# Output projection of a two-layer Conformer/attention trunk: the order of its three passes, and one load of the attention half's weights for two of them

## The chip, the cores and the metric

The kernel runs on one core of a Trainium2 chip. The metric is the device time of one execution in microseconds (us). A core has five engines, each with its own instruction queue that is worked off in order: TensorE (PE, matrix products into the PSUM banks, with its weight loads shown apart as PEld), VectorE (DVE), ScalarE (ACT), GpSimd (POOL) and SyncE (SP, which here only issues DMA transfers). They wait for each other through semaphores.

## The reference

Two layers, 512 tokens, model width 1024. What matters here is the middle of each layer, where the channels of two groups (512 conv channels, 512 attention channels) are joined and projected back to the model width, and the norm and feed-forward block behind it:

```python
for l in range(DEPTH):
    x = x + 0.5 * swiglu(rms_norm(x, ffn1_norm[l]), ...)
    h = rms_norm(x, mix_norm[l])
    a, g, q, k, v = jnp.split(h @ w_in[l], splits, axis=-1)
    conv_out = conv_module(a, g, conv_w[l], conv_b[l], conv_norm[l])
    ...
    diff_out = diff_attention(q, k, v, rel_bias, lam, lam_init, subln_norm[l])
    x = x + jnp.concatenate([conv_out, diff_out], axis=-1) @ w_out[l]
    x = x + 0.5 * swiglu(rms_norm(x, ffn2_norm[l]), ...)
```

`w_out` is 1024 x 1024; its rows 0 to 511 meet the conv channels, rows 512 to 1023 the attention channels. Everything is float32.

## The kernel before

**Layout.** Activations lie transposed: channels on the 128 partitions, tokens along the free dimension. `x` is 8 tiles of 128 channels x 512 tokens, kept on the chip throughout. Attention works through 4 blocks of 128 queries, from block 3 down to block 0 (`steps`, line 932), each block over 4 heads.

**Split products.** Float32 operands are split into a high part of reduced precision (`F32R`) and the remainder, and a product is three matmuls (`mm3`, lines 198 to 204): high x high, high x low, low x high. A raw weight tile of 128 x 512 is loaded into the ring `wraw` (5 entries) by SP, its high part is written by ACT into the ring `whi` and the remainder by DVE or POOL into `wlo` (9 entries each; `parts_of`, lines 99 to 103). `chunk` (line 105) loads and splits two such tiles. In the output projection the remainder is POOL's (the argument `G`, line 1046), and each entry holds the weights of exactly one output tile of 128 channels in one half: the chunk `m // 2`, its entry `m % 2`.

**Order.** The kernel is written against a planner, which follows the written order as a priority, assigns a ring entry or a PSUM bank when an instruction that needs one is placed, and fixes the order of every engine's queue from its own estimate of times. Later work can so be placed ahead of earlier work that isn't ready.

**Around the change.** Attention's last steps (`attend`, line 1008) are, per block: the heads' products with the values (`values`, line 974), squares on ACT (983), a reduction on DVE (985), an addition and a power on POOL (986, 260), scaling on DVE (989), four transposes on PE (1001), and the high and low part of the result into `acth` and `actl` (ACT 1003, DVE 1004). `conv_finish` (line 919) writes the conv channels into tiles 0 to 3 of the same two arrays (POOL 924, ACT 926, DVE 927, ACT 928, DVE 929); attention's four heads are tiles 4 to 7.

The output projection (lines 1042 to 1056) then makes three passes over the eight output tiles `m`: the attention half for tokens 256 to 511 (blocks 2 and 3), the conv half for all tokens, the attention half for tokens 0 to 255 (blocks 0 and 1). Each pass loads and splits its own weights, four chunks, so that those of the attention half are loaded twice. Every output tile of a pass is 4 x 3 matmuls into a bank called `ps_out` (tags `sc` and `po` by turns, two banks each), 256 or 512 columns wide, and an addition on DVE into `x` (line 1051).

`after(m)` prepares tile `m` of `x` for the next norm (`Prep.tile`, line 306: high part on ACT into `acth`, low part on DVE into `actl`, the square on ACT, its sum on DVE). It overwrites tile `m` of `acth` and `actl`, which the projection reads, and so follows the last pass that reads that tile: tiles 0 to 3 are prepared during the third pass, 4 to 7 after it. `first_products` (line 339, called at line 1095) then takes the eight tiles in the order 0 to 7.

Of the kernel before, what the change touches and what calls it, by code (L numbers as in the profile page):

```python
# [20 lines left out]
SEQ = 512  # L21
DM = 1024
KT = DM // P
# [25 lines left out]
    ((10, 18, 15, 19, 16, 20, 17, 21), "last"),  # L49
)  # L50
ORDER = (0, 4, 1, 5, 2, 6, 3, 7)

POOL_TAPS = (TAPS, 0, 0, 10)

# [16 lines left out]
def trunk(ctx: ExitStack, tc: tile.TileContext, xt, par, lamv, relb, onehot,  # L71
          gu1, dn1, wag, wqkv, wout, gu2, dn2, out):
    nc = tc.nc
    V, S, G, T = nc.vector, nc.scalar, nc.gpsimd, nc.tensor
# [14 lines left out]
    def bank(tag, name):  # L89
        return psum.tile([P, 512], F32, tag=tag, name=name, bufs=BANKS[tag])  # L90
# [4 lines left out]
    def ring(tag, n=512):  # L95
        dt = F32R if tag in ("whi", "wlo") else F32
        return wp.tile([P, 512], dt, tag=tag, name=tag, bufs=RING[tag])[:, :n]

    def parts_of(raw, eng=None):
        hi, lo = ring("whi", raw.shape[-1]), ring("wlo", raw.shape[-1])  # L100
        S.activation(hi, raw, AF.Copy)  # L101
        (eng or V).tensor_tensor(out=lo, in0=raw, in1=f32(hi), op=ALU.subtract)  # L102
        return hi, lo

    def chunk(src, eng=None):
        w = []
        for n in range(2):
            raw = ring("wraw")
            nc.sync.dma_start(raw, src[:, n * 512 : (n + 1) * 512])
            w.append(parts_of(raw, eng))  # L110
        return w

    def wpart(w, b, n=P):
        hi, lo = w[b * n // 512]
        c = b * n % 512
        return hi[:, c : c + n], lo[:, c : c + n]
# [31 lines left out]
    class Sums:  # L148

        def __init__(self, load, n=512):  # L150
            self.load, self.n, self.r, self.w = load, n, {}, {}
            for k, first in (("u2u1", "u2"), ("g1u1", "g1")):
                self.r[k] = ring("wsum", n)
                self.get(first, self.r[k], pin=True)
                self.get("u1", self.r[k], add=True)
# [42 lines left out]
    def mm3(ps, w, x, start, stop, pin=False):  # L198
        (wh, wl), (xh, xl) = w, x
        first = T.matmul(ps, wh, xh, start=start, stop=False)  # L200
        if pin:
            tc.keep_in_program_order(first)
        T.matmul(ps, wh, xl, start=False, stop=False)  # L203
        T.matmul(ps, wl, xh, start=False, stop=stop)  # L204
# [58 lines left out]
    def rows_rstd(s, dim, use="", pin=False):  # L263

        ps = bank("y", "ps_rows")
        for j in range(NT):
            mm = T.transpose(ps[:, j * P : (j + 1) * P], s[:, j * P : (j + 1) * P], ident)
            if pin:
                tc.keep_in_program_order(mm)
        v = small.tile([P, NT], F32, tag=f"rowv{use}", name="rowv")  # L270
        V.tensor_reduce(v, ps.rearrange("p (j c) -> p j c", j=NT), axis=AX.X, op=ALU.add)
        V.tensor_scalar(v, v, 1.0 / dim, EPS, op0=ALU.mult, op1=ALU.add)
        return rsqrt(v, NT, use), v
# [24 lines left out]
    class Prep:  # L298


        def __init__(self, l, gain):
            self.l, self.gain = l, gain
            self.hi, self.lo = acth, actl
            self.s = tmp.tile([P, SEQ], F32, tag="ssum", name="ssum", bufs=1)

        def tile(self, k, square=True):
            g = col(self.l, self.gain, k)
            S.activation(self.hi[:, k, :], x[:, k, :], AF.Copy, scale=g)
            V.scalar_tensor_tensor(
                self.lo[:, k, :], x[:, k, :], g, f32(self.hi[:, k, :]), op0=ALU.mult, op1=ALU.subtract  # L310
            )
            if square:
                self.square(k)

        def square(self, k):
            if k == 0:
                S.activation(self.s, x[:, k, :], AF.Square)
            else:
                sq = tmp.tile([P, SEQ], F32, tag="sq", name="sq")
                S.activation(sq, x[:, k, :], AF.Square)  # L320
                V.tensor_tensor(self.s, self.s, sq, op=ALU.add)
# [17 lines left out]
    def first_products(pr, w, ps, early=False, tail=None):  # L339


        if not early:
            rc, v = rows_rstd(pr.s, DM)
            r = spread(rc, "rb", split=True)
        ks = ORDER if tail else range(KT)
        for at, k in enumerate(ks):
            if tail and at == TAIL_AT:
                tail()
            if early and not tail and at == STATS_AT:
                rc, v = rows_rstd(pr.s, DM, pin=True)  # L350
            for i in range(2):
                mm3(ps[0][i], wpart(w[0][i], k), pr[k], at == 0, at == KT - 1,
                    pin=early and (at in (0, STATS_AT) or tail))
        for i in range(2):
            for at, k in enumerate(ks):
                if tail and at == i == 0:
                    rc, v = rows_rstd(pr.s, DM, pin=True)
                if early and i == 0 and at == STATS_AT + (2 if tail else 0):
                    r = spread(rc, "rb", pin=True)
                mm3(ps[1][i], wpart(w[1][i], k), pr[k], at == 0, at == KT - 1,  # L360
                    pin=early and at in (0, STATS_AT, STATS_AT + 2))
        return rc, v, r
# [221 lines left out]
    def begin(pr, loads, tail=None):  # L584
        ws = [[chunk(src) for src in pair] for pair in loads]
        ps = [pair_banks() for _ in loads]
        return [*zip(ws, ps)], first_products(pr, ws, ps, early=tail is not None, tail=tail)
# [184 lines left out]
    def mixer(l, pr, after, begun):  # L772
        with tc.tile_pool(name="mix", bufs=1) as mp, tc.tile_pool(name="mt", bufs=2) as mt:
# [101 lines left out]
            ch, cl = acth, actl  # L875
# [163 lines left out]

            for half, t in ((1, slice(SEQ // 2, SEQ)), (0, slice(0, SEQ)), (1, slice(0, SEQ // 2))):
                w = [None] * 4
                for m in range(KT):
                    if w[m // 2] is None:
                        w[m // 2] = chunk(wout[l, half, m // 2], G)
                    ps = bank(("sc", "po")[m % 2], "ps_out")[:, : t.stop - t.start]
                    for kk in range(4):
                        k = half * 4 + kk
                        mm3(ps, wpart(w[m // 2], (m % 2) * 4 + kk), (ch[:, k, t], cl[:, k, t]), kk == 0, kk == 3)  # L1050
                    V.tensor_tensor(x[:, m, t], ps, x[:, m, t], op=ALU.add)

                    if half == 1 and t.start == 0 and m < KT // 2:
                        after(m)
            for m in range(KT // 2, KT):
                after(m)


    pr = Prep(0, "ffn1_norm")
    for k in range(KT):  # L1060
# [12 lines left out]
    for l in range(DEPTH):  # L1073
        nxt = {}

        def preparing(gain, l2=l):
            def after(m):
                if m == 0:
                    nxt["p"] = Prep(l2, gain)
                nxt["p"].tile(m)  # L1080
            return after

        def store(m):
            nc.sync.dma_start(out[m], x[:, m, :])

        def store_half(n, half, queue):
            queue.dma_start(out[KT - 1][:, n * HS : (n + 1) * HS], half)

        with tc.tile_pool(name="ffn", bufs=1) as fp:
            begun = ffn(fp, pr, gu1[l], dn1[l], preparing("mix_norm"), begun,  # L1090
                        lambda tail: begin(nxt["p"], [[wag[l, c, i] for i in range(2)] for c in range(2)], tail),
                        (l == 0, 1), aside if l == 0 else None)
        mixer(l, nxt["p"], preparing("ffn2_norm"), begun)
        with tc.tile_pool(name="ffn", bufs=1) as fp:
            begun = begin(nxt["p"], [[gu2[l, m, i] for i in range(2)] for m in range(2)])
            if l + 1 < DEPTH:
                begun = ffn(fp, nxt["p"], gu2[l], dn2[l], preparing("ffn1_norm", l + 1), begun,
                            lambda tail: begin(nxt["p"], [[gu1[l + 1, m, i] for i in range(2)] for m in range(2)], tail), (0, 1))
            else:
                ffn(fp, nxt["p"], gu2[l], dn2[l], store, begun, lambda tail: tail(store_half), (0, 0), end=True)  # L1100
        pr = nxt["p"]
# [74 lines left out]
```

## Time and profile before

| | |
|---|---|
| time, median of 3 runs | 1770.37 us (1769.22 to 1770.41) |
| the profiled execution's own time | 1772.28 us |
| its span, first to last instruction | 1770.5 us |
| output projection of layer 0 in it | about 495 to 544 us from the span's start |
| output projection of layer 1 in it | about 1374 to 1423 us |
| DVE, ACT and POOL busy | 83%, 59% and 29% of the span |
| moved by DMA | 257.79 MB, 146 GB/s on average |

A row of the profile that begins with a line number is a group of instructions of that line of the kernel: engine, operation, tile written <- tiles read, count. The views quoted below are: busy time by window (a stretch in us from the span's start, its length, then for each engine its busy time and the instructions in it, the granted clock of PE as a share, the DMA engines' busy share and GB/s), one tile's instructions (count, least/median/most duration in ns, first and last start in us, shapes), and the timeline (start in us, duration in us). Matmuls overlap in PE's pipeline: a matmul's duration is longer than the pace at which they follow each other. A few matmul records are missing in a trace.

### The profile page before, as it was taken

The page shows a single profiled execution, that of the slowest core. Times are in us where ns is not written, and L with a number is a line of the kernel's source. Part 1 is how long each engine was busy: PE and PEld are TensorE (multiplying, and loading weights), DVE is VectorE, ACT ScalarE, POOL GpSimd, SP SyncE. Part 2 cuts the span into 40 slices and gives each one's busy share as a digit, 9 for nine tenths or more (in the row PEclk, how much of TensorE's full clock was granted, in tenths as well). Part 3 has the DMA queues.
Part 4 walks back from the last instruction along what each step waited for, and adds up shares of the span by engine and source line. Part 5 has one row for each costly group of instructions (what it writes and reads, how often), then busy time and mean ns, then how long its engine had stood idle before and what let it go on. Part 6 is the DMA issues. An engine that isn't in the chain of part 4 may idle for free.

```text
span 1770.5 us, 33000 instructions
## 1 busy us (share of the span) xinstructions
PE 1758.8 (99%) x11852; PEld 1620.9 (92%) x11852; DVE 1470.9 (83%) x2646; ACT 1037.4 (59%) x1955; POOL 516.1 (29%) x497
## 2 busy tenths in 40 slices
PE   9999999999999999999999999999999999999998
PEld 7799999988788899999988999999887888999998
DVE  7969888969877869899977798899698678698887
ACT  6546565755855446566644565666559554465664
POOL 1111112169970011112200121121798600111122
PEclk9999999999999999999999999999999999999999
DMA  7457777533223447677543576776231234576774
GB/s 230 128 140 188 172 194 177 145 112 102 66 84 108 134 123 186 162 202 179 145 142 103 152 182 172 192 162 177 81 113 49 100 105 135 132 184 171 193 179 126
DMA packets 166614, 257.79 MB, mean 146 GB/s; under 512 B 19271, under 2 KB 63318, under 8 KB 166448
## 3 DMA queue, kind: packets, MB, share of 16 engines
q1 hardware_dynamic: 129600, 201.25, 35.3%
q0 software_dynamic: 36416, 54.12, 18.6%
q8 instruction: 93, 1.52, 0.3%
q14 instruction: 73, 0.60, 0.1%
q10 hardware_dynamic: 432, 0.29, 0.1%
HBM read 253.48 MB, written 3.42 MB: 145 GB/s over the span
## 4 chain that ended last, share of the span: by engine, by line
PE 94%; DVE 2%; DMA 1%; POOL 1%; ACT 1%; issue 1%; DVEq 0%; ACTq 0%; SPq 0%; POOLq 0%
PE ps_pair L434 36%; PE ps_pair L523 16%; PE ps_pair L200 9%; PE ps_pair L203 9%; PE ps_pair L204 9%; PE ps_out L200 2%; PE ps_out L203 2%; PE ps_out L204 2%; PE ps_pair L829 2%; PE ps_pair L828 2%; PE ps_pair L827 2%; PE ps_sc L944 1%; PE ps_v L858 1%; PE ps_v L859 1%; PE ps_v L857 1%
## 5 line engine op out<-in xcount | busy, mean ns | idle before, releaser
L101 ACT ACTIVATE whi<-wraw 128x512 fp32r<-128x512 f32 x744 | 452.5, 627 | 409.1 <-PE ps_pair L203 170.0
L102 DVE TENSOR_TENSOR wlo<-wraw,whi 128x512 fp32r<-128x512 f32 x640 | 426.3, 685 | 110.1 <-ACT whi L101 97.5
L160 POOL DMA_DIRECT2D wsum<-in_gu x128 | 112.0, 914 | 701.1 <-DMA wsum<-in_gu 279.2
L434 PE MATMUL ps_pair<-acth,wlo 128*128 128x256 f32 x1024 | 289.8, 283 | 0.0
L434 PE MATMUL ps_pair<-actl,whi 128*128 128x256 f32 x1024 | 289.8, 283 | 0.0
L434 PE MATMUL ps_pair<-acth,whi 128*128 128x256 f32 x1024 | 289.8, 283 | 0.0
L434 PE MATMUL ps_pair<-th,whi 128*128 128x256 f32 x768 | 217.3, 283 | 0.0
L434 PE MATMUL ps_pair<-tl,whi 128*128 128x256 f32 x768 | 217.3, 283 | 0.0
L434 PE MATMUL ps_pair<-th,wlo 128*128 128x256 f32 x768 | 217.3, 283 | 0.0
L200 PE MATMUL ps_pair<-acth,whi 128*128 128x512 f32 x512 | 200.0, 393 | 0.3 <-DVE gs L642 0.3
L203 PE MATMUL ps_pair<-actl,whi 128*128 128x512 f32 x512 | 199.5, 390 | 0.0
L204 PE MATMUL ps_pair<-acth,wlo 128*128 128x512 f32 x512 | 199.3, 390 | 0.0
L434 PEld LDWEIGHTS ps_pair<-actl,whi 128*128 128x128 f32 x1024 | 196.6, 192 | 0.2
L434 PEld LDWEIGHTS ps_pair<-acth,whi 128*128 128x128 f32 x1024 | 196.6, 192 | 0.2
L434 PEld LDWEIGHTS ps_pair<-acth,wlo 128*128 128x128 f32 x1024 | 196.6, 192 | 0.0
L160 POOL DMA_DIRECT2D wsum<-in_dn x112 | 98.8, 1120 | 271.4 <-DMA wsum<-in_dn 46.3
L102 DVE TENSOR_TENSOR wlo<-wsum,whi 128x512 fp32r<-128x512 f32 x192 | 130.0, 683 | 23.7 <-ACT whi L101 23.4
L434 PEld LDWEIGHTS ps_pair<-th,whi 128*128 128x128 f32 x768 | 147.5, 192 | 0.0
L434 PEld LDWEIGHTS ps_pair<-tl,whi 128*128 128x128 f32 x768 | 147.5, 192 | 0.0
L434 PEld LDWEIGHTS ps_pair<-th,wlo 128*128 128x128 f32 x768 | 147.5, 192 | 0.0
L523 PE MATMUL ps_pair<-hh,whi 128*128 128x256 f32 x512 | 145.0, 283 | 1.6 <-ACT keep L530 1.6
L102 POOL TENSOR_TENSOR wlo<-wraw,whi 128x512 fp32r<-128x512 f32 x104 | 137.0, 1339 | 31.2 <-ACT whi L101 19.0
(209 smaller groups left out, 4460.8 us busy)
## 6 DMA issues: line engine op xcount, KB each, us to landing
wraw<-in_gu SPq DMA_DIRECT2D x280, 256.0 KB, 3.4
wsum<-in_gu SPq DMA_DIRECT2D x128, 256.0 KB, 3.8
wsum<-in_gu POOLq DMA_DIRECT2D x128, 256.0 KB, 4.6
wraw<-in_dn SPq DMA_DIRECT2D x68, 256.0 KB, 3.4
wraw<-in_wqkv SPq DMA_DIRECT2D x48, 256.0 KB, 2.6
wraw<-in_wout SPq DMA_DIRECT2D x48, 256.0 KB, 2.7
wraw<-in_dn SPq DMA_DIRECT2D x64, 128.0 KB, 3.7
wraw<-in_wag SPq DMA_DIRECT2D x32, 256.0 KB, 2.9
```

Source lines behind the costliest of these rows:

```text
L101: S.activation(hi, raw, AF.Copy)
L102: (eng or V).tensor_tensor(out=lo, in0=raw, in1=f32(hi), op=ALU.subtract)
L160: nc.gpsimd.dma_start(dst[:, to], src, accum_op=ALU.add)
L200: first = T.matmul(ps, wh, xh, start=start, stop=False)
L203: T.matmul(ps, wh, xl, start=False, stop=False)
L204: T.matmul(ps, wl, xh, start=False, stop=stop)
L434: mm = T.matmul(ps, l, r, start=first and i == j == 0, stop=False, skip_group_check=True)
L523: mm = T.matmul(ps, s[:, f], r, start=side not in self.begun, stop=False, skip_group_check=True)
L827: T.matmul(ps[n], xh[:, t], wh, start=k == 0, stop=False)
L828: T.matmul(ps[n], xh[:, t], wl, start=False, stop=False)
L829: T.matmul(ps[n], xl[:, t], wh, start=False, stop=k == KT - 1)
L857: T.matmul(ps, xh[:, t], wh, start=k == 0, stop=False)
```

## The change

The passes become: the attention half for tokens 256 to 511, the attention half for tokens 0 to 255, the conv half. The dictionary of weights now spans all passes, so the second pass uses the tiles of the first. The conv half takes output tiles 4 to 7 first, then 0 to 3 (`LATER`), and so does `first_products` where it has no `tail`. Tiles 4 to 7 are prepared for the next norm during the conv half, tiles 0 to 3 behind it. Since tile 0 is no longer the first to be prepared, the norm's sum is begun by whichever square comes first, and `preparing` makes its `Prep` at the first call.

```diff
+LATER = (4, 5, 6, 7, 0, 1, 2, 3)
...
             self.s = tmp.tile([P, SEQ], F32, tag="ssum", name="ssum", bufs=1)
+            self.squares = 0
...
         def square(self, k):
-            if k == 0:
+            self.squares += 1
+            if self.squares == 1:
                 S.activation(self.s, x[:, k, :], AF.Square)
...
-        ks = ORDER if tail else range(KT)
+        ks = ORDER if tail else LATER
...
-            for half, t in ((1, slice(SEQ // 2, SEQ)), (0, slice(0, SEQ)), (1, slice(0, SEQ // 2))):
-                w = [None] * 4
-                for m in range(KT):
-                    if w[m // 2] is None:
-                        w[m // 2] = chunk(wout[l, half, m // 2], G)
+            w = {}
+            for half, t in ((1, slice(SEQ // 2, SEQ)), (1, slice(0, SEQ // 2)), (0, slice(0, SEQ))):
+                for m in range(KT) if half else LATER:
+                    if (half, m // 2) not in w:
+                        w[half, m // 2] = chunk(wout[l, half, m // 2], G)
                     ps = bank(("sc", "po")[m % 2], "ps_out")[:, : t.stop - t.start]
                     for kk in range(4):
                         k = half * 4 + kk
-                        mm3(ps, wpart(w[m // 2], (m % 2) * 4 + kk), (ch[:, k, t], cl[:, k, t]), kk == 0, kk == 3)
+                        mm3(ps, wpart(w[half, m // 2], (m % 2) * 4 + kk), (ch[:, k, t], cl[:, k, t]), kk == 0, kk == 3)
                     V.tensor_tensor(x[:, m, t], ps, x[:, m, t], op=ALU.add)
-
-                    if half == 1 and t.start == 0 and m < KT // 2:
+                    if half == 0 and m >= KT // 2:
                         after(m)
-            for m in range(KT // 2, KT):
+            for m in range(KT // 2):
                 after(m)
...
         def preparing(gain, l2=l):
+            made = []
+
             def after(m):
-                if m == 0:
-                    nxt["p"] = Prep(l2, gain)
-                nxt["p"].tile(m)
+                if not made:
+                    made.append(Prep(l2, gain))
+                    nxt["p"] = made[0]
+                made[0].tile(m)
             return after
```

## The prediction

> **What bounds the kernel now.** I read the page's span and busy shares first.
>
> ```profile
> span 1770.5 us, 33000 instructions
> ## 1 busy us (share of the span) xinstructions
> PE 1758.8 (99%) x11852; PEld 1620.9 (92%) x11852; DVE 1470.9 (83%) x2646; ACT 1037.4 (59%) x1955; POOL 516.1 (29%) x497
> ```
>
> TensorE (PE) lacks 11.7 us of being busy for the whole span. Time can be won only by closing one of its gaps, and it is lost at once when a new gap opens. So I went to the stretch that the change touches and asked for the busy time by window. The rows are, for layer 0: the end of attention, the output projection, the opening of the second feed-forward block; and the output projection of layer 1.
>
> ```profile
> core 0: us, PE busy (x) PEld busy (x) DVE busy (x) ACT busy (x) POOL busy (x), PEclk, DMA share, GB/s
> 485.00:495.10 10.10, 9.07 (x65) 7.75 (x65) 9.81 (x41) 8.53 (x30) 5.19 (x6) 1.00 0.01 2
> 495.10:544.05 48.95, 48.90 (x318) 44.49 (x319) 34.48 (x69) 29.90 (x61) 29.53 (x23) 1.00 0.33 108
> 544.07:585.00 40.93, 40.93 (x184) 33.81 (x183) 30.94 (x55) 17.33 (x28) 1.92 (x2) 1.00 0.35 114
> 1374.30:1423.20 48.90, 48.87 (x318) 44.45 (x319) 34.40 (x69) 29.84 (x61) 28.98 (x23) 1.00 0.32 109
> ```
>
> Three things are to be seen. The projection already keeps PE busy for 48.90 of 48.95 us, at full clock. What follows it has no gap at all. And the two layers' projections repeat each other within 0.05 us, with as many instructions on each engine, so one layer's sum may be doubled.
>
> **What the change moves.** The three passes of the projection lie thus in the trace (busy time of the instructions on the tile ps_out alone):
>
> ```profile
> 495.10:511.86 16.76, 15.17 (x103) 1.00 0.14 47
> 511.86:532.55 20.69, 20.50 (x91) 1.00 0.43 140
> 532.55:544.07 11.52, 11.52 (x97) 1.00 0.42 138
> ```
>
> The first is the attention half for tokens 256 to 511, mixed with the last heads of attention; the second is the conv half; the third the attention half for tokens 0 to 255. The change swaps the second and the third. All 288 matmuls stay with their widths: 96 in the third pass, 11.52/96 = 0.12 us each; in the conv half, 20.69 us less 0.35 for four transposes, over 89 = 0.23 us each. **Matmul work: 0.**
>
> **What it removes.** The weights of the attention half are no longer loaded twice: per layer 8 loads of 256 KB, 8 ScalarE splits, 8 GpSimd subtractions.
>
> ```profile
> L101 ACT ACTIVATE whi<-wraw x15: 615/627/632, 498.7 to 529.9; 128x512 fp32r<-128x512 f32 x15
> L102 POOL TENSOR_TENSOR wlo<-wraw,whi x15: 1286/1299/1751, 505.1 to 530.6; 128x512 fp32r<-128x512 f32 x15
> L109 SPq DMA_DIRECT2D wraw<-in_wout x10: 327/328/328, 506.5 to 521.2; - x10
> ```
>
> (From the view of the raw weight tiles between 495 and 532 us; durations are least, median, most in ns.) That is 8 x 0.63 = 5.0 us of ACT, 8 x 1.30 = 10.4 us of POOL and 8 issues of 0.33 us on SP's queue per layer, all inside the windows above in which PE doesn't wait. **On the path: 0.** The cover is PE's own 48.9 us; without it a split would be owed to whoever waited for it, up to 0.63 + 1.30 us, but the rows show nobody.
>
> **What it adds: a wait for the last attention block.** Queries are worked off from block 3 down to block 0, and tokens 0 to 255 need blocks 1 and 0. In the kernel before, the conv half stands between. Block 0's way to its output appears in the view of the tile ps_o (PE's last values product is L974; of L1003 and L1004 the last start counts) and in that of the tile so:
>
> ```profile
> L1001 PE MATMUL ps_o<-ident,ov x4: 270/272/272, 521.2 to 521.5; 128*128 128x128 f32 x4
> L974 PE MATMUL ps_o<-vv,at x2: 270/272/273, 510.2 to 510.3; 128*128 128x128 f32 x2
> L1003 ACT ACTIVATE acth<-ps_o,gsub x2: 669/679/689, 510.5 to 521.8; 128x512 fp32r<-128x512 f32 x2
> L1004 DVE SCALAR_TENSOR_TENSOR actl<-ps_o,gsub,acth x2: 736/744/751, 512.3 to 522.5; 128x512 fp32r<-128x512 f32 x2
> L974 PEld LDWEIGHTS ps_o<-vv,at x1: 187/187/187, 510.2 to 510.2; 128*128 128x128 f32 x1
> L983 ACT ACTIVATE sq<-ps_o x1: 579/579/579, 512.7 to 512.7; 128x512 f32<-128x512 f32 x1
> L989 DVE TENSOR_TENSOR ov<-ps_o,rs_y x1: 692/692/692, 518.7 to 518.7; 128x512 f32<-128x512 f32 x1
> ```
>
> ```profile
> L985 DVE TENSOR_REDUCE so<-sq x1: 671/671/671, 513.7 to 513.7; 128x4 f32<-128x512 f32 x1
> L986 POOL TENSOR_TENSOR so<-so,se x1: 198/198/198, 517.4 to 517.4; 128x4 f32<-128x4 f32 x1
> L260 POOL TENSOR_TENSOR rs_y<-so,mhalf x1: 1006/1006/1006, 517.7 to 517.7; 128x4 f32<-128x4 f32 x1
> ```
>
> Block 0 is ready at 522.5 + 0.75 = 523.3 us, 11.4 us after the conv half began and 9.2 us before its consumer starts: hidden now. But much of that way is queueing which the change takes away. POOL was at this, by its timeline,
>
> ```profile
> 505.13 12.31 POOL L102 TENSOR_TENSOR wlo<-wraw,whi 128x512 fp32r<-128x512 f32 x8
> ```
>
> when the reduction ended at 513.7 + 0.7 = 514.4, and L986 stood 3.0 us behind it. Those eight weights are split later in the new order, since the ring of nine split weight tiles keeps eight for their second use until pass two runs. L983 began 2.1 us after L974's end (510.6), L1001 1.8 us after L989's (519.4). The durations from L983 to L1003 alone add to 0.58 + 0.67 + 0.20 + 1.01 + 0.69 + 0.6 + 0.69 = 4.4 us. With ordinary hand-overs the way can be read off block 2, before POOL's run (L983's first start, L1004's last):
>
> ```profile
> L1004 DVE SCALAR_TENSOR_TENSOR actl<-ps_o,gsub,acth x2: 748/748/749, 488.3 to 496.0; 128x512 fp32r<-128x512 f32 x2
> L983 ACT ACTIVATE sq<-ps_o x2: 586/586/587, 488.8 to 496.5; 128x512 f32<-128x512 f32 x2
> L989 DVE TENSOR_TENSOR ov<-ps_o,rs_y x1: 681/681/681, 492.5 to 492.5; 128x512 f32<-128x512 f32 x1
> L1003 ACT ACTIVATE acth<-ps_o,gsub x1: 687/687/687, 494.4 to 494.4; 128x512 fp32r<-128x512 f32 x1
> ```
>
> From 488.8 to 495.1 are 6.3 us to the high part, to 496.7 are 7.9 us to the low one. Put behind L974's end at 510.6: ready at 516.9 and 518.5 as the late end. The early end is the bare 4.4 us, with the last head as much earlier as the conv matmuls that PE ran before it took (next paragraph, 1.6 us): 510.6 - 1.6 + 4.4 = 513.4.
>
> **What PE has to do meanwhile.** The view of ps_out for the first-pass window holds
>
> ```profile
> L200 PE MATMUL ps_out<-acth,whi x35: 278/283/682, 495.2 to 511.5; 128*128 128x256 f32 x32, 128*128 128x512 f32 x3
> L203 PEld LDWEIGHTS ps_out<-actl,whi x34: 188/192/192, 497.2 to 511.5; 128*128 128x128 f32 x34
> L203 PE MATMUL ps_out<-actl,whi x34: 280/283/401, 497.3 to 511.6; 128*128 128x256 f32 x32, 128*128 128x512 f32 x2
> L204 PEld LDWEIGHTS ps_out<-acth,wlo x34: 187/191/192, 497.4 to 511.6; 128*128 128x128 f32 x34
> L204 PE MATMUL ps_out<-acth,wlo x34: 279/283/396, 497.5 to 511.7; 128*128 128x256 f32 x32, 128*128 128x512 f32 x2
> ```
>
> Seven conv matmuls, the 512-wide ones (7 x 0.23 = 1.6 us), are in it: the planner already takes ready conv work ahead of unfinished attention work, and gives it an output bank. It can do so afterwards too, but only for one output tile of twelve matmuls: each output tile uses one ring entry, and eight of nine are held. So PE has 511.86 + 5 x 0.23 = 513.0, and with L1001's transposes (0.35 of pace) 513.35 us. A second conv tile comes after a split of 0.63 + 1.30 us in the freed entry, from about 514.9 on, if the planner puts it there.
>
> **The gap.** PE is free at 513.35; the high part is ready between 513.4 and 516.9: 0 to 3.6 us. The low part follows 1.6 us later by block 2's rows; the first matmul of each of four open output tiles (0.12 us each) covers 0.5 us, so up to 1.1 us more. Per layer 0 to 4.7 us. I take 2.4: nearer the middle, because the hand-overs of block 2 apply, while the freed ACT and POOL let the last head finish earlier. What is queued behind the wait are pass two, the rest of the conv splits (their entries come free tile by tile), and everything after; nothing of it is shortened later, so PE's gap goes to the end. DVE's evictions and the norms have slack.
>
> **What is late or early next.** In the second pass, conv weights are split as entries free, every 1.44 us, against POOL's 1.30: seven by its end, and PE then takes one per 2.7 us. **0.** At the end, the conv half's output tiles leave every 2.7 us instead of 1.44, so DVE's work for the next norm (add, two preparations, one weight split, about 0.7 us each, 2.8 together) spreads wider. Tiles 0 to 3 must wait for the last conv matmul, as tiles 4 to 7 now wait for the last attention matmul; the products take them in the order 4 to 7, 0 to 3, four tiles (5.4 us) later. There was no gap (40.93 of 40.93 us), so **0** either way. The counters in the norm code change which square is written first, not how many.
>
> [...] The longest idle time of PE in this trace is in these windows,
>
> ```profile
> 1751.30:1753.40 2.10, 0.03 (x1) 0.00 (x0) 2.04 (x4) 2.07 (x5) 0.00 (x0) 1.00 0.05 10
> 1753.40:1760.00 6.60, 6.58 (x55) 6.58 (x55) 6.42 (x13) 2.32 (x5) 0.00 (x0) 1.00 0.20 79
> ```
>
> and the clock granted after it is 1.00. [...]
>
> **The sum.** 0 + 0 + 2 x 2.4 = +4.8 us: profiled execution 1772.28 (span 1770.5 and 1.8 around it) becomes 1777.1. That execution stands 1.9 us above the median of the runs shown, 1770.37, so the forecast is 1770.4 + 4.8 = 1775.2 us; with the ends, 1770.4 to 1779.8.
>
> **Rivals.** *Hidden after all: not slower.* The last head's values product is planned earlier, since ACT's splits between 498 and 514 are gone, or the second conv tile fills the gap. Mechanism: block 0 is ready by 513.9, a gap of 0.5 us or less, 2 x 0.5 = +1.0: 1771.4. It decides from 0.2% (3.5 us, about what a measurement of this kernel tells from no change), that is a gap under 1.75 us per layer. For it: the queueing counted above. Against: 6.3 us in the only undisturbed block.
>
> *No filler: much slower.* Pass two's four output tiles hold all four banks while they wait, or no conv weights are split in time. PE then stops at 511.86 - 1.6 + 0.35 = 510.6, block 0 comes at 516.9 - 1.6 = 515.3, low part 1.1 beyond the cover: 5.8 us per layer, +11.6: 1782.0. [...] Against it: the seven early conv matmuls.
>
> *Faster.* It could come only from gaps in these windows: 10.10 - 9.07 and 48.95 - 48.90 are 1.08 us per layer, 2.2 in all, so 1768.2 at best; the ones before 495.1 lie ahead of anything that changes. Over 0.2% would need gaps elsewhere, such as the 2.1 us above, to close by a different plan.
>
> **How the numbers follow.** Forecast (gap of 1.75 to 4.7 us) 0.50; hidden or equal 0.31; no filler 0.12; faster by over 0.2% 0.07. Slower by over 0.2% is 0.50 + 0.12 = 0.62, within 0.31, faster 0.07. The likeliest case's own range is 1773.9 to 1779.8. The range for 8 in 10 leaves the faster case and the upper part of the no-filler case out, half in ten each: 1769.0 to 1783.0.
>
> **What would show it.** Right: in both layers a PE gap before the first 256-wide matmul of the second pass, ended by ACT's L1003 (high part) or DVE's L1004; some twelve 512-wide matmuls ahead of it; POOL idle before L986; 32 loads of in_wout in all; no gap after the pass order's end. Wrong on filler: no 512-wide ps_out matmul before the gap. Wrong altogether: PE busy through the second pass's start, or a gap at the conv half or at the next block's first products, which I price at nothing.

## The result, and the profile after

| | before | after |
|---|---|---|
| median of 5 runs each, taken together | 1769.22 us (1768.66 to 1770.41) | 1782.06 us (1781.27 to 1783.26) |
| ratio after to before, 95% interval | | 1.0071 [1.0059, 1.0082] |
| profiled execution | 1772.28 us | 1781.82 us |

The change costs 12.8 us. The busy shares of the changed kernel:

```profile
span 1780.0 us, 32900 instructions
## 1 busy us (share of the span) xinstructions
PE 1763.6 (99%) x11852; PEld 1625.2 (91%) x11852; DVE 1469.8 (83%) x2646; ACT 1034.1 (58%) x1939; POOL 492.6 (28%) x481
```

ACT and POOL have 16 instructions fewer each (the splits of both layers), PE as many as before. PE's busy time is nevertheless 4.8 us longer: some matmuls took longer than they did before. It isn't one execution's accident: the mean granted clock of the changed kernel is 0.996 or 0.997 in each of its five runs, and 0.999 or 1.000 in every later run of the kernel before.

Busy time by window, in the columns shown in the prediction: for each layer the projection, then the opening of the next feed-forward block.

```profile
495.60:550.60 55.00, 50.76 (x318) 46.15 (x319) 36.68 (x75) 28.92 (x57) 17.36 (x15) 0.97 0.21 68
550.60:591.50 40.90, 40.90 (x183) 33.80 (x182) 31.13 (x55) 17.56 (x29) 2.84 (x3) 1.00 0.38 115
1379.05:1434.90 55.85, 51.62 (x320) 46.77 (x321) 37.02 (x76) 29.25 (x57) 17.36 (x15) 0.94 0.21 69
1434.90:1475.90 41.00, 41.00 (x184) 33.91 (x183) 31.20 (x55) 17.33 (x28) 2.84 (x3) 1.00 0.39 113
```

All of the loss is in the projection. From its first matmul to the first one of the next block it now takes 54.96 us in layer 0 (495.67 to 550.63) and 55.48 us in layer 1, where it took 48.91 us in both. That is 6.05 + 6.57 = 12.6 of the 12.8 us. The feed-forward block opens without a gap, as before. Two things are new in the projection's rows: 4.2 us in which PE isn't busy, and a granted clock of 0.97 and 0.94.

PE's timeline of layer 0, from the end of the first pass to the first matmuls of the second (start, duration, and in brackets the idle time before and what ended it):

```profile
510.64 0.28 PE L205 MATMUL ps_out<-acth,wlo 128*128 128x256 f32 x1
514.31 0.63 PE L1004 MATMUL ps_o<-ident,ov 128*128 128x128 f32 x4 [3.39 <-DVE ov L992]
515.72 1.22 PE L201 MATMUL ps_out<-acth,whi 128*128 128x256 f32 x4 [0.78 <-ACT acth L1006]
516.74 0.41 PE L204 MATMUL ps_out<-actl,whi 128*128 128x256 f32 x1
```

PE runs dry at 510.92 and waits twice: 3.39 us for block 0's scaled values (its lines are three higher now: 989 is 992, 1001 is 1004, 1003 is 1006), then, behind the four transposes, 0.78 us for the high part. No 512-wide matmul stands before or between. A matmul lasts 0.28 us where the next would have followed after 0.12, so each gap costs some 0.16 us more than its idle time: 3.55 + 0.94 = 4.5 us. Layer 1 has the same two gaps, 3.39 and 0.78 us.

The other part of the loss is the clock. These rows are cut where the granted clock changes, and at the same spacing before:

```profile
508.91:512.33 3.42, 2.01 (x18) 1.81 (x16) 3.05 (x7) 1.90 (x3) 0.59 (x2) 1.00 0.00 0
512.33:515.74 3.41, 0.65 (x5) 0.44 (x5) 0.98 (x3) 0.69 (x1) 1.11 (x1) 1.00 0.02 5
515.74:519.15 3.41, 3.41 (x16) 3.41 (x17) 0.71 (x1) 0.04 (x1) 0.00 (x0) 0.50 0.00 0
519.15:522.57 3.42, 3.42 (x30) 3.42 (x30) 1.27 (x3) 1.86 (x3) 2.61 (x3) 1.00 0.09 32
...
1392.96:1396.38 3.42, 1.40 (x12) 1.20 (x11) 3.06 (x6) 1.45 (x3) 1.20 (x2) 1.00 0.00 0
1396.38:1399.79 3.41, 1.26 (x5) 0.89 (x6) 0.88 (x2) 0.69 (x1) 0.50 (x1) 0.50 0.00 0
1399.79:1403.21 3.42, 3.42 (x17) 3.42 (x18) 0.56 (x1) 0.20 (x1) 0.00 (x0) 0.50 0.00 0
```

Just when block 0 has come, the clock is halved for 3.41 us: 16 matmuls go through where the next window takes 30. In layer 1 it is halved for two such windows, in the first of which PE was mostly idle anyway. The projection's extra time less the gaps puts the half clock at 6.05 - 4.5 = 1.6 us in layer 0 and 6.57 - 4.5 = 2.1 us in layer 1, a short wait for the low part among it. So the sum of the loss is 2 x 4.5 us for the gaps and 3.6 us for the clock; the run "Warm through the gap" below gives some 0.6 of the 3.6 us back to the waits.

Why did nothing fill the gap? The order in which PE executed the projection's matmuls tells it, read from the timelines of layer 0 (width, count and pass; attention's own matmuls are left out). A view names the operands, not the number of an output tile.

```
before                                  after
(pass one goes on)                      (pass one goes on)
512 x1   conv half, at 504.95           256 x12  pass one, at 509.25
256 x12  pass one                       (idle 3.39, block 0's transposes, idle 0.78)
512 x1   conv half, at 506.62           256 x4   pass two, at 515.72, the first
256 x12  pass one, at 507.11                     matmuls of four output tiles
512 x5   conv half                      256 x92  pass two
256 x12  pass one, at 510.35            512 x96  conv half, at 528.84
512 x89  conv half, at 511.86
256 x96  third pass, at 532.55
```

What follows is read off the kernels, and the next two runs test it. Banks of one tag are handed out in the written order. In the kernel before, the conv half was the written next user of `sc`, so its first tile got a bank while 36 matmuls of pass one, three output tiles' worth, were still to come. In the changed kernel the written next users of all four banks are tiles 0 to 3 of pass two. They take them and wait for block 0, and the conv half stands behind them, its first tile too, which the next run shows to be ready.

### The profile page after: what moved, and what is told of

Its sections match the earlier page's. It is cut to its first block, busy times and chain, and to the rows that moved or that the text cites. A ratio compares the mean times of both kernels' runs of the same rounds, so it can differ in the third digit from the quotient of the medians.

```text
span 1780.0 us, 32900 instructions
## 1 busy us (share of the span) xinstructions
PE 1763.6 (99%) x11852; PEld 1625.2 (91%) x11852; DVE 1469.8 (83%) x2646; ACT 1034.1 (58%) x1939; POOL 492.6 (28%) x481
## 5 line engine op out<-in xcount | busy, mean ns | idle before, releaser
L102 ACT ACTIVATE whi<-wraw 128x512 fp32r<-128x512 f32 x728 | 444.1, 628 | 410.8 <-PE ps_pair L204 172.6
L526 PE MATMUL ps_pair<-hl,whi 128*128 128x256 f32 x512 | 144.9, 283 | 0.0
L526 PE MATMUL ps_pair<-hh,wlo 128*128 128x256 f32 x512 | 144.9, 283 | 0.0
```

The costliest lines, as they stand in the source:

```text
L526: mm = T.matmul(ps, s[:, f], r, start=side not in self.begun, stop=False, skip_group_check=True)
```

## The experiments

In the expectations, A is the theory held at that time, and the other letters are its rivals, with the numbers that each would give. The kernel before was run again with each of the three groups: 1769.97 us (18 runs; bank, written, warm and reload), 1769.74 us (17 runs; two tiles, shared only and the kernel before) and 1769.61 us (21 runs; the last two).

**One conv tile with a bank of another tag.** The changed kernel, but the conv half's first tile takes the idle bank `y` instead of its turn for `sc`.

```diff
-                    ps = bank(("sc", "po")[m % 2], "ps_out")[:, : t.stop - t.start]
+                    tag = "y" if half == 0 and m == KT // 2 else ("sc", "po")[m % 2]
+                    ps = bank(tag, "ps_out")[:, : t.stop - t.start]
```

> The changed kernel with one edit: the conv half's first output tile (m = 4) takes the bank y instead of sc. Theory A (banks handed out in written order keep conv work out of the gap): PE works off 12 conv matmuls of 0.227 us, 2.7 us, before block 0 is ready; the 3.39 us gap shrinks to about 0.7 us with the 0.78 us behind it, the granted clock stays 1.00, the loss per layer is 1.5 us: about 1772 us. Rival B (the planner keeps written order, or the conv half isn't ready): order and time unchanged, 1782 us.

Measured: 1773.98 us, ratio 1.002 [1.0011, 1.0029]: 8.1 us are won back by a name of a bank. Its PE timeline at the same place:

```profile
513.09 0.39 PE L205 MATMUL ps_out<-acth,wlo 128*128 128x512 f32 x1
514.09 0.66 PE L1004 MATMUL ps_o<-ident,ov 128*128 128x128 f32 x4 [0.61 <-DVE ov L992]
515.52 0.74 PE L201 MATMUL ps_out<-acth,whi 128*128 128x256 f32 x4 [0.78 <-ACT acth L1006]
```

The filler that the prediction had counted on, twelve 512-wide matmuls, now stands ahead of the transposes. PE runs on to 513.48, where the prediction had 513.0. Gaps of 0.61 and 0.78 us are left, the clock stays full (behind the gaps of layer 0 a 256-wide matmul lasts 0.28 us, where the changed kernel had 0.41), and the projection takes 51.08 us in both layers. The time is 2 us above the expectation; the two gaps, 0.61 + 0.78 + 2 x 0.16 = 1.7, are most of the 2.2 us per layer that remain.

**One conv tile written ahead of pass two.** The same filler by the other way: its bank stays `sc`, but its turn comes earlier.

```diff
-            for half, t in ((1, slice(SEQ // 2, SEQ)), (1, slice(0, SEQ // 2)), (0, slice(0, SEQ))):
-                for m in range(KT) if half else LATER:
+            for half, t, ms in ((1, slice(SEQ // 2, SEQ), range(KT)), (0, slice(0, SEQ), LATER[:1]),
+                                (1, slice(0, SEQ // 2), range(KT)), (0, slice(0, SEQ), LATER[1:])):
...
+                for m in ms:
...
```

The lines left out keep the preparation of that tile for the next norm behind pass two.

> The changed kernel with conv output tile m = 4 written ahead of the second pass, in its usual bank. Theory A: its turn for a bank of sc comes before the second pass's, so it fills the gap as in the run with bank y: about 1772 us. Rival B (conv not ready in time, its inputs or weights late): PE waits for conv first, 1780 us or more.

Measured: 1774.28 us, ratio 1.0025 [1.0015, 1.0035], with the same 51.08 us in both layers. In the first run the written order stayed and a bank was free; in this one the banks stayed and the turn came earlier. Either is enough, so what the conv tile lacked was a bank at its turn, and neither its inputs nor its weights.

**Warm through the gap.** The changed kernel, with twelve matmuls of a constant into another bank behind the first pass; nothing reads their result. They do no work of the projection, but keep PE busy.

```diff
+                if t.start:
+                    idle = bank("tp", "ps_idle")
+                    with behind(mm):
+                        for _ in range(12):
+                            T.matmul(idle, ones_r, ones_r.unsqueeze(1).broadcast_to([P, NT, P]), start=True, stop=True)
```

Here `mm` is the last matmul of the first pass.

> The changed kernel with 12 matmuls on constants (512 wide, 0.227 us each, 2.7 us, their result unused) behind the first pass. They do no work of the kernel, so the wait for block 0 stays. Theory A (the gap of 3.39 us is paid once, and half clock for 3.4 us in layer 0 and 6.8 us in layer 1 is paid on top): granted clock 1.00 throughout, 1.7 + 3.4 = 5.1 us less: 1777 us. Rival C (the half clock falls on time that PE would have waited anyway): 1782 us.

Measured: 1780.03 us (1778.94 to 1782.14), ratio 1.0057 [1.0045, 1.007], between the two expectations. The profiled execution is the slowest of the five. In it layer 0 kept its clock and took 53.91 us instead of 54.96; layer 1 lost it for one window and took 55.40 instead of 55.48. The windows of layer 1:

```profile
1396.75:1400.17 3.42, 1.84 (x11) 1.23 (x11) 1.44 (x2) 0.69 (x1) 0.08 (x1) 1.00 0.00 0
1400.17:1403.59 3.42, 3.42 (x18) 3.42 (x18) 0.42 (x1) 0.63 (x1) 0.66 (x1) 0.50 0.00 0
```

Block 0 comes no sooner here: its transposes start 514.94 - 496.14 = 18.80 us after the projection's first matmul in layer 0, against 514.31 - 495.67 = 18.64 us in the changed kernel. The half clock is thus a cost of its own. The other four runs bear it out: their mean granted clock is 1.000, where a single window at half clock (half of 3.41 us, of some 1780) would leave 0.999, and they took 1778.94 to 1780.85 us, by their median 2.3 us less than the changed kernel. The expectation had set the cost too high, and had taken for granted that the clock would be kept in both layers of every run.

The size comes out below 3.6 us, too. Layer 0, at full clock, still takes 53.91 - 48.91 = 5.0 us more than before, 0.16 of them by the later transposes. So the waits alone cost some 4.8 us per layer instead of 4.5. The 0.3 between is mostly PE's wait for the low part:

```profile
516.34 0.74 PE L201 MATMUL ps_out<-acth,whi 128*128 128x256 f32 x4 [0.78 <-ACT acth L1006]
517.13 0.39 PE L204 MATMUL ps_out<-actl,whi 128*128 128x256 f32 x1
```

The first matmul with the low part starts 0.79 us after the first with the high part, and the four of the high part fill only 4 x 0.12 = 0.48 of it. In the changed kernel it starts 1.02 us after (516.74 less 515.72), of which the four fill 0.85 at half clock: the slower pace hides a part of that wait. By this estimate, from one layer of one execution, the half clock costs 6.05 - 4.8 = 1.2 and 6.57 - 4.8 = 1.8 us, 3.0 in all.

**The new order with the weights loaded anew.** The changed kernel, but each pass loads and splits its own weights, as before.

```diff
             for half, t in ((1, slice(SEQ // 2, SEQ)), (1, slice(0, SEQ // 2)), (0, slice(0, SEQ))):
+                w = {}
```

> The changed kernel, but each pass loads and splits its own weights again (24 loads per layer, no tile held for two passes). Theory A (the order of the passes is the cause, the shared load no part of it): the gap stays, and POOL's splits for the second pass again stand before block 0's small operations, up to 5 us later per layer: 1782 to 1795 us. Rival D (keeping eight of nine ring entries is what stops the conv half from filling in): 1769 to 1773 us.

Measured: 1793.97 us, ratio 1.0136 [1.0121, 1.0152]: the loss is the order's, and sharing the weights takes half of it away. PE's and POOL's timelines:

```profile
519.31 1.09 PE L1004 MATMUL ps_o<-ident,ov 128*128 128x128 f32 x4 [8.52 <-DVE ov L992]
521.17 1.22 PE L201 MATMUL ps_out<-acth,whi 128*128 128x256 f32 x4 [0.78 <-ACT acth L1006]
```

```profile
505.15 10.95 POOL L103 TENSOR_TENSOR wlo<-wraw,whi 128x512 fp32r<-128x512 f32 x7
516.06 0.20 POOL L989 TENSOR_TENSOR so<-so,se 128x4 f32<-128x4 f32 x1
```

The gap is 8.52 us, because block 0's small addition on POOL stands behind seven splits. This is the queueing that the prediction saw before the change (L986, 3.0 us behind such a run) and expected to go; it goes only with the second load.

**Two conv tiles as filler.** The changed kernel with tiles 4 and 5 in banks `y` and `tp`, and three ring entries of their own for the conv half's weights (the third argument of `chunk`, handed on to `parts_of`).

```diff
...
-                        w[half, m // 2] = chunk(wout[l, half, m // 2], G)
-                    ps = bank(("sc", "po")[m % 2], "ps_out")[:, : t.stop - t.start]
+                        w[half, m // 2] = chunk(wout[l, half, m // 2], G, None if half else mp)
+                    tag = {4: "y", 5: "tp"}.get(m) if half == 0 else None
+                    ps = bank(tag or ("sc", "po")[m % 2], "ps_out")[:, : t.stop - t.start]
```

> The changed kernel with two conv output tiles free to fill the wait: tile 4 takes bank y, tile 5 bank tp, and the conv half's split weights have three ring entries of their own. Theory A (all of the change's loss is PE's missing work while block 0 is unfinished): 24 conv matmuls, 5.4 us, cover the 3.4 + 0.8 us, no gap over 0.8 us in the projection, clock 1.00: 1769.5 to 1771 us, the time before. Rival B (something else of the change costs time too, at its end or through the wider output tiles): as with one tile, 1773 us or more.

Measured: 1775.05 us, ratio 1.003 [1.0019, 1.004]. A miss: with twice the filler no better than with one tile.

```profile
517.99 0.60 PE L1007 MATMUL ps_o<-ident,ov 128*128 128x128 f32 x4
519.37 0.74 PE L204 MATMUL ps_out<-acth,whi 128*128 128x256 f32 x4 [0.78 <-ACT acth L1009]
```

The planner put all 24 conv matmuls ahead of block 0's transposes, so the 3.39 us are closed, but nothing is left for the 0.78 us behind them. By the medians 1775.05 - 1769.74 = 5.3 us are lost: 2 x (0.78 + 0.16) = 1.9 in this gap, and 3.0 that the next run loses, too.

**Shared weights alone.** The order of before, but the attention half's weights loaded once, and the conv half's in three entries of their own (in the passes' loop `w = {}` once, the key `(half, m // 2)`, and the third argument of `chunk` as above).

> The kernel before, its order of passes unchanged, with the weights of the attention half loaded once for both of its passes and three ring entries of their own for the conv half. It does what the change removes, without what it adds. Theory A (the 16 loads, 16 ACT splits and 16 POOL subtractions lie under busy PE): 1769 to 1771 us, no difference. Rival E (they cost time on the path, about 0.3 us per split weight tile where PE waits): 1765 us or less.

Measured: 1772.77 us, ratio 1.0016 [1.0007, 1.0025], 3.0 us more than the kernel before. A miss by 2 us. POOL's timeline around block 2:

```profile
480.14 2.53 POOL L105 TENSOR_TENSOR wlo<-wraw,whi 128x512 fp32r<-128x512 f32 x2
482.61 2.65 POOL L902 TENSOR_TENSOR yp<-yp,prod 128x512 f32<-128x512 f32 x2
...
493.33 0.21 POOL L989 TENSOR_TENSOR so<-so,se 128x4 f32<-128x4 f32 x1
```

With free entries, two more splits are placed in the midst of attention, where DVE, ACT and POOL have work that PE waits for. That this is the cause wasn't shown by this run. The theory after it: the entries cost something only where their splits are made early.

**The kernel before once more.** One more execution, because the first profile has gaps of 1.58 us near 1099 and 2.09 us near 1751, the second of them quoted in the prediction.

> The kernel before once more, unchanged. Theory A (the two gaps of 2.09 us and 1.58 us in its first profile belong to that execution, not to the plan): they are gone or elsewhere and the time is near 1770 us. Rival F (they are planned waits that the change removed): both are there again and the time is near 1772 us.

Measured: 1768.83 us. Its windows at both places, and those of the first profile:

```profile
1095.00:1103.00 8.00, 8.00 (x69) 8.00 (x68) 7.31 (x14) 4.51 (x10) 1.76 (x2) 1.00 0.82 209
1740.00:1757.00 17.00, 16.65 (x139) 16.45 (x138) 13.18 (x24) 7.22 (x15) 3.31 (x4) 1.00 0.56 131
```

```profile
1095.00:1103.00 8.00, 6.42 (x54) 6.22 (x53) 5.00 (x10) 3.80 (x8) 1.97 (x3) 1.00 0.80 179
1740.00:1757.00 17.00, 14.91 (x125) 14.71 (x123) 11.58 (x20) 5.86 (x13) 3.57 (x4) 1.00 0.56 134
```

Both gaps belong to that one execution, not to the kernel; what made them wasn't followed up. Together, 3.67 us, they are about what the first profile took more than this one (1772.28 less 1768.83 is 3.45). Held against this execution, the changed kernel's profiled one takes 1781.82 - 1768.83 = 13.0 us more, as the medians say; against the first it is only 9.5.

**Two tiles, with their work held back.** The changed kernel with tiles 4 and 5 in `y` and `tp` and one entry for tile 5's weights; its split is held behind `conv_finish`'s first tanh on ACT and last scaling on POOL, and tile 5's last six matmuls behind block 0's transposes (`done` holds these instructions, and `entry` loads and splits one weight tile instead of two).

```diff
...
+                        two = (done["S"], done["G"]) if (half, m) == (0, 5) else ()
+                        with behind(*two):
+                            w[half, m] = entry(wout[l, half, m // 2], m % 2, two and spare("c"))
+                    tag = {4: "y", 5: "tp"}.get(m) if half == 0 else None
...
+                        with behind(*([done["T"]] if (half, m) == (0, 5) and kk > 1 else [])):
+                            mm3(ps, wpart([w[half, m]], kk), (ch[:, k, t], cl[:, k, t]), kk == 0, kk == 3)
```

> The changed kernel with two conv output tiles in the wait again (banks y and tp), but only one more weight entry, whose split is held back until attention's softmaxes are done, and with the last six conv matmuls held back until block 0's transposes. Theory A (the change loses only PE's missing work; the run with three early entries lost 0.9 us per layer in attention and 0.8 us behind the transposes): no gap over 0.3 us in the projection, attention as before, 1769.5 to 1771.5 us. Rival B (the order costs something else as well): 1773 us or more.

Measured: 1770.11 us, ratio 1.0003 [0.9994, 1.0011]. The whole loss is gone. The projections of both layers:

```profile
495.00:549.00 54.00, 53.86 (x342) 48.54 (x342) 41.19 (x84) 31.55 (x62) 17.88 (x16) 1.00 0.25 75
1374.00:1428.00 54.00, 54.00 (x341) 48.70 (x342) 40.24 (x79) 31.05 (x60) 17.43 (x15) 1.00 0.26 79
```

No gap is left but 0.14 us ahead of layer 0's first matmul, which the kernel before has, too, and the projections take 48.92 and 48.97 us, as before the change.

**Shared weights, with their splits held back.** The order of before, the weights shared, and the conv half's first splits in own entries held back in the same way.

> The kernel before with the attention half's weights loaded once, and three entries of their own for the conv half, whose first splits are held back until attention's softmaxes are done. Theory A (the removed loads and splits lie under busy PE, and the 3 us of the run with early splits came from those splits in attention): 1769 to 1771 us, no difference from before. Rival E (removing them is worth time): under 1767 us. Rival G (keeping the weights costs time in itself): 1772 us or more, as with the early splits.

Measured: 1770.27 us, ratio 1.0004 [0.9995, 1.0013]. POOL's timeline around block 2 shows what is different from the run above without the hold:

```profile
478.89 3.98 POOL L904 TENSOR_TENSOR yp<-yp,prod 128x512 f32<-128x512 f32 x3
...
491.36 0.20 POOL L991 TENSOR_TENSOR so<-so,se 128x4 f32<-128x4 f32 x1 [0.44 <-DVE so L990]
```

The two splits are gone from the midst of attention, block 2's addition comes 2.0 us sooner, and the projections of the two layers end at 544.80 and 1422.38 us instead of 546.08 and 1424.82: 2.44 us by the second, against 2.50 in the medians. So the early splits are the likely cause there; the two kernels differ besides in that this one loads and splits one weight tile at a time and leaves the conv half's first tile in the common ring. With nothing in its way, the removed work is worth nothing that these runs can tell: no version is faster than the kernel before, whose PE has no gap left to close in the projection.

## Why the prediction was right in its direction and wrong in its size

The forecast was 1775.2 us, +4.8; it became 1782.06, +12.8, near the upper end of the range.

- **Bound by PE: right.** Every loss and every recovery was a gap or a clock of PE.
- **Matmul work 0, removed loads and splits 0: right.** The count of matmuls is the same; the order of before with shared weights stands at 1.0004 [0.9995, 1.0013].
- **The way of block 0, 4.4 to 6.3 us: right, at its late end.** From the view of the tile ps_o between 509 and 516 us of the changed kernel (the last start counts for L977 and L1006):

```profile
L1006 ACT ACTIVATE acth<-ps_o,gsub x2: 687/688/688, 509.1 to 515.0; 128x512 fp32r<-128x512 f32 x2
L977 PE MATMUL ps_o<-vv,at x2: 272/274/275, 509.1 to 509.2; 128*128 128x128 f32 x2
```

From 509.2 + 0.27 to 515.0 + 0.69 are 6.2 us. In it POOL's power took 1.50 us, where the sum of the bare durations had 1.01. POOL was idle before block 0's addition, as foreseen, and its next splits come much later:

```profile
511.66 0.20 POOL L989 TENSOR_TENSOR so<-so,se 128x4 f32<-128x4 f32 x1 [6.58 <-DVE so L988]
511.94 1.50 POOL L261 TENSOR_TENSOR rs_y<-so,mhalf 128x4 f32<-128x4 f32 x1
519.82 9.67 POOL L103 TENSOR_TENSOR wlo<-wraw,whi 128x512 fp32r<-128x512 f32 x7 [6.38 <-ACT whi L102]
```

- **What PE has to do meanwhile: the step that failed.** "the planner already takes ready conv work ahead of unfinished attention work, and gives it an output bank. It can do so afterwards too". It could not. The seven early conv matmuls had their bank in its written turn; after the change the turn belongs to four tiles that wait. The prediction counted ring entries carefully and didn't ask who is next for the banks. PE was free at 510.92 instead of 513.35, and the prediction's own sign of it came true: no 512-wide matmul of ps_out before the gap. Giving one conv tile a bank, or an earlier turn, moved the time to 1774.0 and 1774.3 us, close to the forecast whose filler this is.
- **The gap, 2.4 us per layer: too small through that step**, 3.39 + 0.78 us of idle time in each layer. With the filler given back the loss is 51.08 - 48.91 = 2.2 us per layer, so the rest of this term was sized well.
- **The end, 0: right.** 40.90 of 40.90 and 41.00 of 41.00 us busy behind the projection.
- **The clock: no term of the sum, but a cost.** The granted clock fell to 0.50 in both layers at the 3.39 us gap: from 515.74 us for 3.41 us in layer 0, behind it, and from 1396.38 us for 6.83 us in layer 1, within it. By the estimates above the half clock cost 1.2 to 1.6 us in layer 0 and 1.8 to 2.1 in layer 1. The 2.1 us of idle PE that the prediction quotes from the first profile had left the clock at 1.00.
- **The rival "no filler", at 0.12, is what happened**, by the mechanism that it names. Its 1782.0 is right partly by offsetting errors: it put the gap at 5.8 us per layer, where it is 4.5 to 4.8, and left out the clock, which brought the rest. That the forecast's range holds the result is owed to this rival, not to the mechanism that the forecast priced. How far the rival reaches above its 1782.0, and so the end of the range at 1783.0, is the author's estimate; no run shows it. The runs took 1781.27 to 1783.26 us, with the waits and the half clock as sized above.

## What to carry to other kernels

Work that is ready fills a wait only if everything that it needs comes to it in its turn: before counting on a filler, find who is written next for its PSUM bank, its ring entries and its queue, and whether that one is itself waiting. Reordering a projection so that its last-ready input is wanted sooner took 12.8 us here, all of it repaired by two filler tiles, half of the second held back for the second, short wait; but the repair only returns to the old time, since PE had been full. Entries that allow work earlier also let it collide earlier: the same spare weight entries cost 3.0 us with their splits placed freely, and nothing that the runs can tell with the splits held behind the work that PE was waiting for.

## What the runs showed of the hardware that was not expected

In the changed kernel the granted clock fell to 0.50 at 515.74 and at 1396.38 us, and was 1.00 again 3.41 us later in layer 0 (519.15) and 6.83 us, twice as much, later in layer 1 (1403.21). The falls don't stand at one distance from the start of the gap: 4.82 us after PE ran dry in layer 0 (510.92), and 2.02 us after it in layer 1 (1394.08 + 0.28 = 1394.36). The windows of this section are 3.41 us long, like the shorter of the two stretches. That the clock goes by windows of this length one after the other is the author's estimate from these two stretches, and the borders of the windows far from a change rest on it. Seen so, PE need not be idle throughout a window for the next one to be at half clock. In the changed kernel windows in which PE was busy for 1.40, 0.65 and 1.26 us were each followed by a window at 0.50, and in the warmed kernel one with 1.84 us; the one with 2.01 us was followed by one at 1.00. Two more that kept the full clock, of the kernel with the conv tile written ahead (with the window behind it), and of the kernel before at its own gap:

```profile
1392.86:1396.27 3.41, 2.02 (x11) 1.23 (x10) 1.75 (x4) 1.32 (x2) 2.28 (x2) 1.00 0.00 0
1396.27:1399.68 3.41, 3.35 (x27) 3.15 (x28) 1.03 (x2) 0.63 (x1) 0.54 (x1) 1.00 0.25 77
```

```profile
1749.23:1752.64 3.41, 2.10 (x18) 1.90 (x16) 1.28 (x3) 1.95 (x4) 0.00 (x0) 1.00 0.31 59
```

But busy time alone doesn't draw the border. Near the end of the kernel with two conv tiles a window with 1.73 us kept the full clock behind it, less than the 1.84 us that lost it:

```profile
1767.59:1771.01 3.42, 1.73 (x15) 1.52 (x13) 2.08 (x4) 0.00 (x0) 0.00 (x0) 1.00 0.21 78
1771.01:1773.19 2.18, 0.00 (x0) 0.00 (x0) 0.00 (x0) 0.00 (x0) 0.00 (x0) 1.00 0.34 118
```

A matmul's duration is longer than its pace (0.28 against 0.12 us for one 256 wide), so a window of several short bursts, as the one with 1.84 us, shows more busy time for the same work. What decides whether the clock is kept stays open; no run was made for it. The same gap of 3.39 us lies differently in the windows of the two layers: in layer 0 PE was busy for 2.01 and 0.65 us of two, and one at 0.50 followed; in layer 1 for 1.40 and 1.26 us, of which the second was at 0.50 itself, and one more followed.
